# A transformer encoder on one core: a new cost table and a new rating for the planner that fixes every engine's order

## The chip, the cores and the metric

The kernel runs on one core of a Trainium2 chip. A core has five engines that each take their instructions strictly in the order of the program: PE (TensorE, the matrix engine, with PEld for its weight loads), DVE (VectorE), ACT (ScalarE), POOL (GpSimd) and SP (SyncE, which here only issues transfers). They run beside each other and wait for each other by semaphores. The metric is the device time of one execution in microseconds (us).

## The reference

Two transformer layers on 512 tokens of width 1024, all in float32. Layer 0 mixes tokens by two-dimensional neighbourhood attention, layer 1 by three groups of dilated windowed attention whose outputs are merged by their softmax denominators. Both layers then have a SwiGLU block of hidden width 2816.

```python
for layer in range(DEPTH):                       # DEPTH = 2
    h = rms_norm(x, norm_mix_pre[layer])
    if layer % 2 == 0:
        h = neighbourhood_attention(h, na_w_qkv[j], na_w_o[j], na_rpb[j])
    else:
        h = dilated_attention(h, dil_w_qkv[j], dil_w_o[j])
    x = x + rms_norm(h, norm_mix_post[layer])
    h = rms_norm(x, norm_ffn_pre[layer])
    x = x + rms_norm((silu(h @ w_gate) * (h @ w_up)) @ w_down, norm_ffn_post[layer])
```

## The kernel before

A float32 matrix product is made of three products in the faster type float32r: each operand is split into a high part, `h`, and a remainder, `l` (function `split`, lines 370 to 373: ACT copies the operand to `h` at line 371, DVE subtracts it to get `l` at line 372). `mm3` (lines 381 to 387) then issues `h` by `h` (line 383), `h` by `l` (line 384) and `l` by `h` (line 385). Nearly all of PE's work is on these three lines. The large products are done by a scheme of seven block products instead of eight (class `Seven`, from line 418), whose sums of weights are made on POOL and DVE (lines 451 to 457) and whose results ACT and DVE collect from the accumulators. A row of the profile such as `gu<-rxa,h_b` is a matmul of the gate and up product (`gate_up`), `yd` one of the down product (`down`), `yo` one of the output projection, `vp` and `vd` make the values, `pp` queries and keys, `tr` are transposes of the normalized tokens (lines 599 to 608: four transposes on PE, then ACT at line 607 and DVE at line 608 copy high part and remainder), `s`, `sa`, `sb` are attention scores and `o` their products with the values.

The stages follow each other in time: tokens and values of layer 0, its attention heads (to about 210 us), output projection (to 255 us), gate and up product (to about 490 us), down product (to 593 us), values of layer 1 (to about 705 us), its heads (to about 1080 us), output projection, gate and up, down (to the end).

The order on every engine is not the order in which the code is written. When all instructions are recorded, class `Order` builds the graph of what must wait for what, plays the program through with a table of durations (`_cost`: how long an instruction keeps its engine and how long until its result is there; transfers share one pipe) and takes at each moment the ready instruction of lowest rank (`run`). `pin` repeats this forward and backward eight times, each turn with the ranks of the last, keeps the turn whose played end is earliest, and ties every engine's instructions together in that order (`add_manual_dep`). On the chip each engine then follows its list: if the head of the list waits, all behind it wait too. SP's and POOL's transfers are in such lists as well.

## Time and profile before

| | us |
|---|---|
| three runs, lowest, median, highest | 1476.14, 1478.42, 1480.89 |
| the profiled execution | 1475.85 |
| its span, first to last instruction | 1474.0 |
| PE busy | 1425.7 (97%) |
| DVE busy | 1200.5 (81%) |
| ACT busy | 902.7 (61%) |
| POOL busy | 541.4 (37%) |

The profiled execution is the one from which all durations are read; 1.85 us of its time lie around its span. A row of the timeline gives start and length of an instruction, and in brackets how long its engine had been idle before it and whose result ended the wait. The ends of matmuls are modelled: in a run of matmuls of 256 columns the starts are 0.113 us apart, while each is drawn as about 0.28 us long. An idle time of PE is therefore one that is seen beyond that overlap.

### The profile page before, as it was taken

The page shows a single profiled execution, that of the slowest core. Times are in us where ns is not written, and L with a number is a line of the kernel's source. Part 1 is how long each engine was busy: PE and PEld are TensorE (multiplying, and loading weights), DVE is VectorE, ACT ScalarE, POOL GpSimd, SP SyncE. Part 2 cuts the span into 40 slices and gives each one's busy share as a digit, 9 for nine tenths or more (in the row PEclk, how much of TensorE's full clock was granted, in tenths as well). Part 3 has the DMA queues.
Part 4 walks back from the last instruction along what each step waited for, and adds up shares of the span by engine and source line. Part 5 has one row for each costly group of instructions (what it writes and reads, how often), then busy time and mean ns, then how long its engine had stood idle before and what let it go on. Part 6 is the DMA issues. An engine that isn't in the chain of part 4 may idle for free.

```text
span 1474.0 us, 27934 instructions
## 1 busy us (share of the span) xinstructions
PE 1425.7 (97%) x10788; PEld 1317.0 (89%) x10788; DVE 1200.5 (81%) x1876; ACT 902.7 (61%) x1819; POOL 541.4 (37%) x398
## 2 busy tenths in 40 slices
PE   7999999899999999999999999999999999999997
PEld 7988877899999888999999999989877999999886
DVE  5489976799999788797789788787656989998877
ACT  4478773555555567544467777876675655555664
POOL 5345424644231001566555443334303743330001
PEclk9999999999999999999999999999999999999999
DMA  5356578778333664435433243343665688844662
GB/s 201 133 181 166 164 254 220 257 207 233 115 111 116 206 223 165 159 128 196 139 106 99 86 147 108 108 135 102 221 203 219 207 222 263 262 150 151 192 218 97
DMA packets 86645, 253.22 MB, mean 172 GB/s; under 512 B 19312, under 2 KB 31600, under 8 KB 84464
## 3 DMA queue, kind: packets, MB, share of 16 engines
q1 hardware_dynamic: 77696, 197.69, 40.4%
q0 software_dynamic: 8672, 53.48, 14.0%
q8 instruction: 85, 1.39, 0.4%
q14 instruction: 48, 0.39, 0.1%
q10 hardware_dynamic: 144, 0.26, 0.0%
HBM read 229.24 MB, written 68.29 MB: 202 GB/s over the span
## 4 chain that ended last, share of the span: by engine, by line
PE 66%; DVE 15%; ACT 8%; DMA 4%; issue 4%; POOL 1%; SPq 0%; POOLq 0%; DVEq 0%; ACTq 0%
PE gu L383 7%; PE gu L384 7%; PE gu L385 7%; PE pp_d L383 4%; PE pp_d L385 4%; PE pp_d L384 3%; PE yd_s L385 3%; PE yd_s L384 3%; PE yd_s L383 3%; PE yd_pp L384 2%; PE yd_pp L385 2%; PE yd_pp L383 2%; PE yo L383 2%; PE yo L385 1%; PE yo L384 1%
## 5 line engine op out<-in xcount | busy, mean ns | idle before, releaser
L591 POOL TENSOR_TENSOR rs_yd<-v_yd,mhalf 128x1 f32<-128x1 f32 x8 | 9.5, 1184 | 255.2 <-DVE v_yd L589 255.2
L383 PE MATMUL gu<-rxa,h_c 128*128 128x256 f32 x352 | 99.3, 282 | 3.1 <-DVE memc L845 1.4
L384 PE MATMUL gu<-rxa,h_b 128*128 128x256 f32 x352 | 98.9, 281 | 2.2 <-DVE rxa L608 2.2
L383 PE MATMUL gu<-rxc,h_a 128*128 128x256 f32 x352 | 97.7, 279 | 2.4 <-ACT h_a L371 1.5
L383 PE MATMUL gu<-rxa,h_b 128*128 128x256 f32 x352 | 98.6, 281 | 1.2 <-ACT rxa L607 1.2
L384 PE MATMUL gu<-rxc,h_a 128*128 128x256 f32 x352 | 98.0, 279 | 1.1 <-DVE rxc L608 1.0
L385 PE MATMUL gu<-rxa,l_b 128*128 128x256 f32 x352 | 98.6, 280 | 0.3 <-DVE l_b L372 0.3
L384 PE MATMUL gu<-rxa,h_c 128*128 128x256 f32 x352 | 97.5, 277 | 0.0
L385 PE MATMUL gu<-rxc,l_a 128*128 128x256 f32 x352 | 97.3, 277 | 0.0
L385 PE MATMUL gu<-rxa,l_c 128*128 128x256 f32 x352 | 97.1, 277 | 0.0
L371 ACT ACTIVATE rxc<-mem 128x512 fp32r<-128x512 f32 (+2 forms) x90 | 55.7, 624 | 62.7 <-PE yd_pp L384 31.6
L451 POOL TENSOR_TENSOR r_d<-r_d 128x512 f32<-128x512 f32 x24 | 33.4, 1391 | 162.2 <-DVE l_ad L372 123.5
L451 POOL TENSOR_TENSOR r_gu<-r_gu 128x512 f32<-128x512 f32 x20 | 29.8, 1488 | 148.9 <-DVE l_a L372 105.8
L372 DVE TENSOR_TENSOR rxc<-mem,rxc 128x512 fp32r<-128x512 f32 (+2 forms) x90 | 64.3, 717 | 17.3 <-ACT rxc L371 17.1
L451 POOL TENSOR_TENSOR raw<-raw 128x512 f32<-128x512 f32 x24 | 40.3, 1678 | 94.0 <-DVE l_a L372 66.6
L383 PEld LDWEIGHTS gu<-rxa,h_c 128*128 128x128 f32 x352 | 66.1, 188 | 5.9 <-DVE memc L847 2.0
L384 PEld LDWEIGHTS gu<-rxa,h_b 128*128 128x128 f32 x352 | 67.3, 191 | 2.4 <-DVE rxa L608 2.4
L383 PEld LDWEIGHTS gu<-rxc,h_a 128*128 128x128 f32 x352 | 65.9, 188 | 3.4 <-ACT h_a L371 2.1
L1244 ACT ACTIVATE mem<-mem 128x256 f32<-128x256 f32 x128 | 63.7, 503 | 8.1 <-DVE mem L1243 7.9
L383 PEld LDWEIGHTS gu<-rxa,h_b 128*128 128x128 f32 x352 | 67.0, 191 | 1.6 <-ACT rxa L607 1.4
L384 PEld LDWEIGHTS gu<-rxc,h_a 128*128 128x128 f32 x352 | 66.2, 188 | 1.8 <-DVE rxc L608 1.8
L385 PEld LDWEIGHTS gu<-rxa,l_b 128*128 128x128 f32 x352 | 67.3, 191 | 0.5 <-DVE l_b L372 0.5
(609 smaller groups left out, 6149.6 us busy)
## 6 DMA issues: line engine op xcount, KB each, us to landing
wsum<-wd POOLq DMA_DIRECT2D x24, 1408.0 KB, 11.9
r_d<-dil_qk SPq DMA_DIRECT2D x48, 512.0 KB, 4.1
raw<-wg SPq DMA_DIRECT2D x24, 512.0 KB, 5.7
raw<-wu SPq DMA_DIRECT2D x24, 512.0 KB, 8.2
wsum<-wsum POOLq DMA_DIRECT2D x8, 1408.0 KB, 9.1
raw<-wsum SPq DMA_DIRECT2D x22, 512.0 KB, 4.1
r_gu<-wg SPq DMA_DIRECT2D x20, 512.0 KB, 3.8
r_gu<-wu SPq DMA_DIRECT2D x20, 512.0 KB, 5.8
```

Source lines behind the costliest of these rows:

```text
L371: act.activation(h, src, AF.Copy)
L372: dve.tensor_sub(l, src, h.bitcast(F32))
L383: i = pe.matmul(o, s[0], m[0], start=start, stop=False, skip_group_check=True)
L384: pe.matmul(o, s[0], m[1], start=False, stop=False, skip_group_check=True)
L385: pe.matmul(o, s[1], m[0], start=False, stop=stop, skip_group_check=True)
L451: self.added = e[0].tensor_add(q[0], q[0], q[2])
L591: pool.tensor_tensor(r, v, mhalf, op=ALU.pow)
L1244: act.activation(pr[:, f], pr[:, f], AF.Exp, bias=st[:, c:c + 1], scale=-1.0, accum_out=st[:, c + 2:c + 3])
```

## The change

The change is in the planner alone; no instruction is added or taken away (PE 10,388 matmuls, DVE 1,878 rows, ACT 1,582, SP 520 transfers in both programs).

- `_cost`: a float32r matmul of n columns keeps PE for 17n/38.4 + 3 ns instead of n/2.4 + 13 ns: 116.3 instead of 119.7 for 256 columns, 229.7 instead of 226.3 for 512.
- `access`: two writes of one engine to ranges that interleave, less than 12 instructions apart, keep their written order.
- `usual` is new: it plays a finished order strictly (every engine takes its list as it stands) three times, each time with landings of transfers drawn at random and small random delays of all other results, and returns the mean end.
- `pin` makes 14 turns instead of 8, rates each by `usual` instead of by its one played end, and then goes through the program in stretches of 100 us: in each it tries the ranks of the eight next best turns for that stretch, and keeps them when the rating falls.

```diff
@@ -87,13 +88,12 @@
     if t == "InstDMACopy":
         adds = "bypass" not in str(getattr(i, "cce_op", "bypass"))
         size = 4 * n * outs[0].ap[0][1] * (1.78 if adds else 1)
-
-        return 350 if e == 4 else 1000 if adds else 560, LATE if size < 2e4 else 0, e == 3, 0, size
+        return 350 if e == 4 else 1000 if adds else 560, 0, e == 3, 0, size
     if e == 0:
         if i.is_transpose:
             return (109, 240, False, 1, 0) if srcs[1].ap[0][1] == P else (202, 330, False, 2, 0)
         if str(srcs[0].dtype).endswith("float32r"):
-            return n / 2.4 + 13, n / 2.4 + 175, False, 0, 0
+            return n * 17 / 38.4 + 3, n * 17 / 38.4 + 175, False, 0, 0
 
         upper = outs[0].offset >= HD * 512 if outs[0].ap[0][1] == HD else srcs[1].offset >= HD * srcs[1].tensor.shape[1]
         return 0.75 * n + 15, 1.67 * n + 200, False, 4 if upper else 3, 0
@@ -171,7 +171,9 @@
                 if bank and (self.engine[m] or self.engine[n]):
                     self.pred[n].add(m)
                 elif q0 < p1 and p0 < q1 and lo2 < hi and lo < hi2 and \
-                        any(x < d and c < y for x, y in runs for c, d in runs2):
+                        (any(x < d and c < y for x, y in runs for c, d in runs2) or
+
+                         write and wrote and self.engine[m] == self.engine[n] and n - m < 12):
                     self.pred[n].add(m)
                     if write and len(runs) == 1 and p0 <= q0 and q1 <= p1 and lo <= lo2 and hi2 <= hi:
                         continue
@@ -218,7 +220,7 @@
             for m in before:
                 self.succ[m].append(n)
 
-    stay = 1000.0
+    stay, strict = 1000.0, False
 
     def run(self, rank, back):
 
@@ -242,8 +244,10 @@
                 heap = min((q for q in heaps[e] if q), key=lambda q: q[0])
 
                 for q in heaps[e][3:] if kind == 3 else heaps[e][kind:kind + 1]:
-                    if e == 0 and q and q[0][0] < heap[0][0] + self.stay:
+                    if e == 0 and not self.strict and q and q[0][0] < heap[0][0] + self.stay:
                         heap = q
+                if self.strict and heap[0][0] != len(order[e]):
+                    continue
                 k = heapq.heappop(heap)[1]
                 taken, later, lock, mode, size = self.costs[k]
                 s = max(now, locked[5 - e]) if lock else now
@@ -278,20 +282,54 @@
                 now = min(q[0] if q is wake else q[0][0] for q in (wake, pending) if q)
         return starts, order, max(s + max(c[1], c[4] and LANDING + c[4] / RATE) for s, c in zip(starts, self.costs))
 
-    def pin(self, tc, times):
-        rank, best = list(range(len(self.all))), None
+    def usual(self, order):
+
+        planned, place, ends = self.costs, [0] * len(self.all), []
+        for q in order:
+            for p, k in enumerate(q):
+                place[k] = p
+        self.strict = True
+        for seed in range(3):
+            r = random.Random(seed)
+            self.costs = []
+            for e, (taken, later, lock, mode, size) in zip(self.engine, planned):
+                if size:
+                    later = r.gauss(300, 700) if size < 4e5 else r.gauss(50, 800)
+                    later *= 1.6 if e == 3 else 1
+                else:
+                    later += r.expovariate(1 / 15)
+                self.costs.append((taken, later, lock, mode, size))
+            ends.append(self.run(place, False)[2])
+        self.costs, self.strict = planned, False
+        return sum(ends) / len(ends)
+
+    def pin(self, tc, times, span):
+        rank, found = list(range(len(self.all))), []
+
+        self.costs = [(t, LATE if 0 < size < 2e4 else later, lock, mode, size) for t, later, lock, mode, size in self.costs]
         for _ in range(times):
             starts, order, end = self.run(rank, False)
-            if best is None or end < best[0]:
-                best = end, order
+            found.append((self.usual(order), end, rank, starts, order))
             starts, _, end = self.run([-s - c[1] for s, c in zip(starts, self.costs)], True)
             rank = [end - s - c[0] for s, c in zip(starts, self.costs)]
-        for q in best[1]:
+        found.sort(key=lambda f: f[0])
+
+        best, end, rank, base, order = found[0]
+        for lo in np.arange(0.0, max(base), span):
+            part = [k for k, s in enumerate(base) if lo <= s < lo + span]
+            for _, _, other, _, _ in found[1:9]:
+                mixed, shift = list(rank), float(np.median([rank[k] - other[k] for k in part]))
+                for k in part:
+                    mixed[k] = other[k] + shift
+                _, new, e = self.run(mixed, False)
+                usual = self.usual(new) if e < end + 3000 else best
+                if usual < best:
+                    best, end, rank, order = usual, e, mixed, new
+        for q in order:
             for m, n in zip(q, q[1:]):
                 tc.add_manual_dep(self.all[n], self.all[m].name,
                                   mybir.DependencyInfo(mybir.DependencyClass.NoSync, mybir.DependencyReason.DATA),
                                   reason="order")
-        return best[0]
 
 
 @with_exitstack
@@ -1444,7 +1482,7 @@
               for n, lo, hi, o, c, side in arenas]
     order = Order(tc.nc.cur_bb.bb.instructions)
     order.link(tags, places, extra)
-    order.pin(tc, 8)
+    order.pin(tc, 14, 1e5)
 
 
 def _blocks(w, cols):
```

Lines of the kernel after stand 38 higher from `encoder_kernel` on: line 372 of before is line 410 there, 608 is 646, 845 is 883, 1318 is 1356.

Where the orders differ: half of PE's instructions stand within 4 places of where they stood, nine tenths within 23; on DVE half within 1 and nine tenths within 6. Counted along PE's two lists, the neighbours of different kind (float32r matmul, transpose, float32 matmul) are 433 before and 415 now. The following are three places of it.

DVE at the start of the gate and up product of layer 0. `tr_o0_3_4` is a transposed operand of the fourth token tile, whose remainder the next matmuls of PE need; `l_b0_1` and `l_c0_1` are remainders of weights; the row of `memc` between them in before (line 842) collects a result. Before:

```order
L372 TENSOR_TENSOR l_c0_0_3079<-r_gu0_0_2857,h_c0_0_3078 128x1024
L608 TENSOR_TENSOR rxa_77<-tr_o0_3_3_2809,rxa_77 128x4x128
L441 MEMSET gu0_1_2895 128x256
L372 TENSOR_TENSOR l_b0_1_3101<-r_gu0_1_2892,h_b0_1_3100 128x1024
L842 TENSOR_TENSOR memc0_2852<-memc0_2852,gu0_2_2929 128x256
L372 TENSOR_TENSOR l_c0_1_3161<-r_gu0_1_2892,h_c0_1_3160 128x1024
L608 TENSOR_TENSOR rxa_77<-tr_o0_3_4_2817,rxa_77 128x4x128
L441 MEMSET gu0_2_2929 128x256
L842 TENSOR_TENSOR memc0_2852<-memc0_2852,gu0_3_2963 128x256
```

and now:

```order
L410 TENSOR_TENSOR l_c0_0_3079<-r_gu0_0_2857,h_c0_0_3078 128x1024
L646 TENSOR_TENSOR rxa_77<-tr_o0_3_3_2809,rxa_77 128x4x128
L646 TENSOR_TENSOR rxa_77<-tr_o0_3_4_2817,rxa_77 128x4x128
L410 TENSOR_TENSOR l_b0_1_3101<-r_gu0_1_2892,h_b0_1_3100 128x1024
L880 TENSOR_TENSOR memc0_2852<-memc0_2852,gu0_2_2929 128x256
L410 TENSOR_TENSOR l_c0_1_3161<-r_gu0_1_2892,h_c0_1_3160 128x1024
L646 TENSOR_TENSOR rxa_77<-tr_o0_3_5_2825,rxa_77 128x4x128
L479 MEMSET gu0_2_2929 128x256
```

The copy of `tr_o0_3_4` moved ahead of the two weight remainders and the collected result between them. On PE the four transposes that it copies moved too: they stood directly ahead of the first matmul that reads them, and now stand 21 matmuls ahead of it.

DVE in the gate and up product of layer 1, at the eighth of its 22 units. The rows that write `memc1` from `gu1_8` collect a result, after which PE may go on in that accumulator. Before:

```order
L372 TENSOR_TENSOR l_a1_12_13729<-raw1_12538,h_a1_12_13728 128x1024
L845 TENSOR_TENSOR memc1_12534<-memc1_12534,gu1_8_13248 128x256
L372 TENSOR_TENSOR vmem_80<-r_gu1_10_13478,vmem_80 128x512
L372 TENSOR_TENSOR l_c1_9_13775<-raw1_12538,h_c1_9_13774 128x1024
L847 TENSOR_TENSOR memc1_12534<-mem_79,gu1_8_13248 128x256
L453 TENSOR_TENSOR r_gu1_10_13478<-r_gu1_10_13478 128x512
L842 TENSOR_TENSOR memc1_12534<-memc1_12534,gu1_11_13598 128x256
```

and now:

```order
L889 TENSOR_TENSOR mem_79<-memc1_12534,mem_79 128x2x256
L883 TENSOR_TENSOR memc1_12534<-memc1_12534,gu1_8_13248 128x256
L410 TENSOR_TENSOR l_a1_12_13729<-raw1_12538,h_a1_12_13728 128x1024
L410 TENSOR_TENSOR vmem_80<-r_gu1_10_13478,vmem_80 128x512
L885 TENSOR_TENSOR memc1_12534<-mem_79,gu1_8_13248 128x256
L491 TENSOR_TENSOR r_gu1_10_13478<-r_gu1_10_13478 128x512
L410 TENSOR_TENSOR l_c1_9_13775<-raw1_12538,h_c1_9_13774 128x1024
```

The row that writes `memc1` from `mem` and `gu1_8` moved ahead of the remainder `l_c1_9`; the row of line 845 (now 883), which collects from the same accumulator into `memc1`, moved in the same way ahead of `l_a1_12`.

SP in the heads of layer 1. `vd0` are stored values that are loaded into a buffer which the heads' last products with the values free; `r_d19` are the weights of a later unit; `sw` are small exchanges of softmax sums. Before:

```order
L1204 DMA sw0_6414<-mem_79 128x16
L1206 DMA mem_79<-sw2_6416 32x4x4
L367 DMA r_d19_10688<-dil_qk 128x1024
L1206 DMA mem_79<-sw2_6416 32x4x4 x3
L367 DMA r_d19_10688<-dil_qk 128x1024
L1206 DMA mem_79<-sw0_6414 32x4x4 x4
L1318 DMA mem_79<-vd0_6418 128x4x256
L1318 DMA mem_79<-vd1_6419 128x1024
```

and now:

```order
L1287 DMA memc0_2852<-dil_bias 128x512
L1242 DMA sw2_6416<-mem_79 128x16
L1356 DMA mem_79<-vd0_6418 128x4x256
L1287 DMA memc0_2852<-dil_bias 128x512
L405 DMA r_d19_10688<-dil_qk 128x1024
L1242 DMA sw0_6414<-mem_79 128x16
L1244 DMA mem_79<-sw2_6416 32x4x4 x4
L405 DMA r_d19_10688<-dil_qk 128x1024
L1244 DMA mem_79<-sw0_6414 32x4x4 x4
```

The load of `vd0` moved from behind both loads of `r_d19` to ahead of them. PE's products with the values that free its buffer (lines 1349 and 1355) moved ahead as well, from behind the matmuls of units 15 to 17 to ahead of them.

## Rows read from the trace of the kernel before

**Rows 1.** The page of the profile: busy time and its share of the span by engine.

```profile
span 1474.0 us, 27934 instructions
PE 1425.7 (97%) x10788; PEld 1317.0 (89%) x10788; DVE 1200.5 (81%) x1876; ACT 902.7 (61%) x1819; POOL 541.4 (37%) x398
```

**Rows 2.** The timeline of PE: the first transposes, and the last matmul (start, length, what, and in brackets the idle time before it).

```profile
7.91 1.97 PE L605 MATMUL tr_a<-ident,mem 128*128 128x128 f32 x8 [7.91 <-DVE mem L598]
...
1465.51 0.39 PE L385 MATMUL yd_s<-h_d1x2b,rxc 128*128 128x512 f32 x1
```

**Rows 3.** The timeline of PE from 276 to 289 us, the start of the gate and up product of layer 0.

```profile
276.16 0.28 PE L383 MATMUL gu<-rxc,h_a 128*128 128x256 f32 x1
276.27 0.28 PE L384 MATMUL gu<-rxc,h_a 128*128 128x256 f32 x1
...
278.20 0.60 PE L605 MATMUL tr_o<-ident,mem 128*128 128x128 f32 x4
279.96 0.50 PE L383 MATMUL gu<-rxa,h_b 128*128 128x256 f32 x2 [1.16 <-ACT rxa L607]
282.69 0.58 PE L384 MATMUL gu<-rxa,h_b 128*128 128x256 f32 x1 [2.23 <-DVE rxa L608]
283.07 0.42 PE L385 MATMUL gu<-rxa,l_b 128*128 128x256 f32 x1
...
288.62 0.30 PE L384 MATMUL gu<-rxa,h_b 128*128 128x256 f32 x1
```

**Rows 4.** The timeline of DVE from 278 to 283 us.

```profile
278.43 1.39 DVE L372 TENSOR_TENSOR l_b<-r_gu,h_b 128x1024 fp32r<-128x1024 f32 x1
279.74 0.41 DVE L842 TENSOR_TENSOR memc<-memc,gu 128x256 f32<-128x256 f32 x1
280.07 1.96 DVE L372 TENSOR_TENSOR l_c<-r_gu,h_c 128x1024 fp32r<-128x1024 f32 x1
281.96 0.68 DVE L608 TENSOR_TENSOR rxa<-tr_o,rxa 128x512 fp32r<-128x512 f32 x1
```

**Rows 5.** The stretch from 282 to 289 us: length, busy time of PE, PEld, DVE, ACT and POOL, then PE's granted clock as a share of full speed, the share of the DMA engines and GB/s.

```profile
282.00:289.00 7.00, 6.31 (x30) 6.31 (x31) 2.78 (x8) 1.44 (x4) 3.51 (x4) 0.53 0.87 298
```

**Rows 6.** The timeline of ACT from 255 to 263 us: the split of a weight that waits for its transfer.

```profile
261.54 1.06 ACT L371 ACTIVATE h_a<-raw 128x1024 fp32r<-128x1024 f32 x1 [1.83 <-DMA raw<-wg]
```

**Rows 7.** Waits of PE in the two gate and up products, from its timeline.

```profile
366.09 0.38 PE L383 MATMUL gu<-rxa,h_c 128*128 128x256 f32 x1 [0.66 <-DVE memc L845]
...
424.42 0.39 PE L383 MATMUL gu<-rxa,h_c 128*128 128x256 f32 x1 [0.42 <-DVE memc L845]
...
472.62 0.38 PE L383 MATMUL gu<-rxa,h_c 128*128 128x256 f32 x1 [0.31 <-DVE mem L845]
...
1245.30 0.39 PE L383 MATMUL gu<-rxa,h_c 128*128 128x256 f32 x1 [1.25 <-DVE memc L847]
```

**Rows 8.** The timeline of DVE ahead of the last of these waits.

```profile
1242.61 2.31 DVE L372 TENSOR_TENSOR l_c<-raw,h_c 128x1024 fp32r<-128x1024 f32 x1
1244.84 0.41 DVE L847 TENSOR_TENSOR memc<-mem,gu 128x256 f32<-128x256 f32 x1
```

**Rows 9.** The timeline in the heads of layer 1, first PE, then DVE.

```profile
959.59 0.39 PE L383 MATMUL pp_d<-rxb,h_cd 128*128 128x256 f32 x1 [1.05 <-DVE mem L689]
...
978.42 0.36 PE L383 MATMUL pp_d<-rxb,h_bd 128*128 128x256 f32 x1 [0.94 <-DVE pp_d L441]
...
975.67 1.87 DVE L372 TENSOR_TENSOR l_cd<-r_d,h_cd 128x1024 fp32r<-128x1024 f32 x1 [0.46 <-ACT h_cd L371]
```

**Rows 10.** The timeline of PE and of DVE at the end of the down product of layer 0.

```profile
593.46 0.36 PE L383 MATMUL vp_d<-h_d,rxa 128*128 128x256 f32 x1
593.66 0.28 PE L384 MATMUL vp_d<-l_d,rxa 128*128 128x256 f32 x1
593.78 0.28 PE L385 MATMUL vp_d<-h_d,rxa 128*128 128x256 f32 x1
...
598.26 0.39 PE L384 MATMUL vp_d<-l_d,rxa 128*128 128x256 f32 x1 [2.03 <-DVE l_d L372]
...
598.12 0.68 DVE L643 TENSOR_TENSOR memc<-yd_s,mem 128x512 f32<-128x512 f32 x1
```

**Rows 11.** The timeline of PE at the end of the heads of layer 1.

```profile
1056.75 0.38 PE L385 MATMUL pp_d<-rxb,l_bd 128*128 128x256 f32 x1 [0.44 <-DVE l_bd L372]
```

**Rows 12.** Two stretches of the gate and up products, columns as in rows 5 (DVE's busy time is the third).

```profile
300.00:350.00 50.00, 50.00 (x443) 50.00 (x442) 48.16 (x55) 25.72 (x45) 26.12 (x18) 1.00 0.84 242
...
1300.00:1350.00 50.00, 49.57 (x423) 48.83 (x422) 48.21 (x65) 27.60 (x49) 13.94 (x8) 1.00 0.37 123
```

**Rows 13.** Line 372 on DVE in the gate and up product of layer 0 (255 to 490 us), by tile: count, shortest, median and longest in ns, first and last start, shape.

```profile
L372 DVE TENSOR_TENSOR l_a<-raw,h_a x12: 1208/1218/1886, 262.6 to 432.4; 128x1024 fp32r<-128x1024 f32 x12
L372 DVE TENSOR_TENSOR l_b<-raw,h_b x12: 1199/1222/2506, 294.4 to 461.8; 128x1024 fp32r<-128x1024 f32 x12
L372 DVE TENSOR_TENSOR l_c<-raw,h_c x12: 1211/2016/2316, 302.3 to 463.9; 128x1024 fp32r<-128x1024 f32 x12
L372 DVE TENSOR_TENSOR l_b<-r_gu,h_b x10: 1202/1226/1391, 272.9 to 474.4; 128x1024 fp32r<-128x1024 f32 x10
```

**Rows 14.** The timeline of SP from 948 to 966 us: its DMA issues (the length is that of the issue).

```profile
953.89 0.38 SPq L367 DMA_DIRECT2D r_d<-dil_qk  x1
...
962.30 2.34 SPq L1318 DMA_DIRECT2D mem<-vd  x3
```

More of the change, by code (lines that the diff above doesn't have):

```diff
@@ L1 @@
 import heapq
+import random
 from contextlib import ExitStack, contextmanager
```

## The prediction

> **What bounds the kernel now.** I read the page first, then PE's timeline, and only then what PE waits for. The page says that PE is busy 1425.7 of 1474.0 us and that DVE, the next engine, has 1200.5 [rows 1]. PE's first instruction starts at 7.91 us and its last matmul ends at 1465.51 + 0.39 = 1465.90 [rows 2], so its idle time between the two is 1465.90 - 7.91 - 1425.7 = 32.3 us. The change leaves every instruction as it is. It can therefore win at most these 32.3 us, and what PE loses at its half clock after long waits. The order within that is all that moves, so the right question is which of PE's waits the new order takes away, and which it makes.
>
> The largest loss is one place, the start of the gate and up product of layer 0. PE waits 1.16 us at 279.96 for ACT, runs two matmuls, and waits 2.23 us at 282.69 for DVE [rows 3]. From 282 to 289 us the granted clock is 0.53, that is the level of 1.2 GHz, behind waits of 3.39 us in sum [rows 5]. The waits in the two gate and up products are of one kind: DVE collects an accumulator (lines 845 and 847) later than PE wants it back [rows 7]. In the last of them DVE was busy with a remainder of 2.31 us before it took the 0.41 us of line 847 [rows 8]. Others stand in the heads of layer 1 [rows 9] and at the end of the down product [rows 10].
>
> **The change, part by part.** All durations are of the one profiled execution: 1475.85 us, 1474.0 of them its span. The median of the three runs is 1478.42, which is 2.57 more; I make the sum against the profiled execution and add 2.57 at the end.
>
> *The start of gate and up, layer 0.* Line 608 for `tr_o0_3_4` started at 281.96, right behind `l_b` (1.39 us), line 842 (0.41) and `l_c` (1.96), 3.76 us of work [rows 4]. Now all three stand behind it, and the four transposes stand 21 matmuls earlier on PE; at 0.11 us a matmul [rows 3] that is 2.3 us, more than the 1.16 us that PE waited for ACT's copy. Both waits go: -3.39. The half clock goes with them, if it was the waits that brought it. From 283.07 to 288.62 PE did 25 matmuls and four transposes in 5.55 us; at full clock these are 25 x 0.11 + 0.60 = 3.35 [rows 3], so another -2.2. Against it: the third unit's first matmuls on `h_a` now stand ahead of eight others that filled PE's wait for that weight. ACT has it at 261.54 + 1.06 = 262.60, released by a transfer [rows 6], and no order makes a transfer earlier; eight matmuls of 0.11 us are +0.9. Together -4.7. The bounds are -5.6 (the eight are hidden) and -1.2 (a wait of 1.3 us remains for the next operand, and the clock falls all the same: -3.39 + 1.3 + 0.9). What is late next: DVE's two remainders, by the 0.68 us of line 608, for matmuls that stand further on.
>
> *Collecting in gate and up, both layers.* The rows of lines 845 and 847 that PE waited for now stand ahead of the weight remainders: 0.66 + 0.42 + 0.31 + 1.25 [rows 7] = -2.6. What hides the remainder's delay of 0.41 us is that it belongs to a unit several matmul groups later; if that cover is gone, the same 0.41 comes back at each place, 1.6 in all. Bounds -2.6 and -1.0.
>
> *Heads of layer 1.* The 0.94 us at 978.42 are a wait for DVE's clearing of `pp_d` (line 441), which stood behind `l_cd`, 1.87 us from 975.67. It now stands ahead of it. The 1.05 us at 959.59 wait for line 689 [rows 9]; 20 matmuls of unit 15 now stand ahead of the waiting one. Together -2.0, bounds -2.0 and 0.
>
> *End of the down product, layer 0.* PE waits 2.03 us for `l_d` [rows 10]. DVE now does line 643 (0.68 us) and one copy of a transpose ahead of `l_d`, while its chain starts some 0.4 us earlier. I keep the wait and count +0.3, bounds -0.5 and +1.4.
>
> *End of the heads.* At 1056.75 PE waits 0.44 for `l_bd` [rows 11]. PE's own work ahead of it shrinks by 2.0 us, DVE's only by the 0.6 us of one row that moved behind: +1.4, bounds 0 and +1.4.
>
> *Changes of kind.* Between matmuls of different kind the starts were 0.20 us apart instead of 0.12 [rows 10]. There are 433 such neighbours before and 415 now: 18 x 0.08 = -1.4 at most. Some lie where PE waits anyway, so I take -1.0.
>
> *The extra rule in `access`* only keeps written orders; it holds back no instruction that PE waits for in these places: 0. *The rest of the order* has small waits that go and others that come. I have priced 10.5 of 32.3 us of idle time; for the other 21.8 I take no change, and a tenth, 2.2 us, to either side.
>
> Sum: -4.7 - 2.6 - 2.0 + 0.3 + 1.4 - 1.0 = -8.6, so 1475.85 - 8.6 = 1467.25 on the profile's scale and 1469.8 on that of the median. I forecast 1470. The bounds added up are -5.6 - 2.6 - 2.0 - 0.5 - 1.4 - 2.2 = -14.3 and -1.2 - 1.0 + 1.4 + 1.4 + 2.2 = +2.8, that is 1464 to 1481.
>
> **The rivals.** *The waits only move.* A wait taken away on PE can come back at the next place, since the transfers and DVE have not become faster; then the idle time stays at 32 us and the time at about 1478. For it speaks that more than half of PE's instructions stand within four places of where they stood, and that DVE in the gate and up products has only 50 - 48.16 = 1.84 us free in 50 [rows 12]. Against it speaks that at 279 to 289 us the engine that was waited for had its work in the wrong order, not too much of it: DVE was busy 2.78 of the 7 us [rows 5].
>
> *SP's queue.* The load of `vd0` now stands ahead of both loads of `r_d19`. Before, it was issued at 962.30, and the first `r_d19` at 953.89 [rows 14]. If `vd0` waits for its buffer as long as before, `r_d19` comes 8.4 us late and all its users with it. PE's products that free the buffer moved ahead, so I take half, 4.2 us, and a stretch at half clock as above, 2.2: 1470 + 6.4 = 1476.4. This counts as no change.
>
> *The slower case: DVE becomes the bound in gate and up.* There DVE has 1.84 and 1.79 us free in 50 [rows 12], so over the 475 us of both products about 17 us. Remainders of one shape take 1.22 us in the median for `l_a` and `l_b` and 2.02 for `l_c` from `raw` [rows 13]: 0.8 us more, which I read as two engines that meet, POOL being busy 26 of these 50 us [rows 12]. The new order moves such pieces against POOL. There are 34 of the short kind in one product, 68 in both [rows 13]. If 40 of them turn long, DVE gets 32 us more work, 15 more than it has free. The 2.6 us of collecting then don't come: 1469.8 + 2.6 + 15 = 1487. It is slower than before from 17 + 8.6 - 2.6 = 23 us of added work, or 29 pieces. Against it: nothing in the order brings these rows nearer to POOL's, and they moved by one place in the median.
>
> The Trainium skill, "SBUF — State Buffer", section "Who interferes with whom", gives a rule for this: VectorE and GpSimd share a port pair that is locked, not shared out, and whoever starts first keeps it for its whole instruction; its section on the two sides of SBUF names a VectorE instruction with two SBUF inputs among those that take it. The trace agrees as far as two lengths of one instruction go, 1.22 and 2.02 us; that the lock is their cause no row here shows. By that rule a change of order alone can lengthen work that nobody added, and the time would be that of the slower case.
>
> *More goes.* If a third of the 21.8 us that I left unpriced goes too, the time is 1470 - 7 = 1463.
>
> **How the numbers follow.** The forecast has 0.54, more goes 0.10, the waits only move 0.16, SP's queue 0.07, DVE as the bound 0.08, and 0.05 are left for new waits behind which the clock falls elsewhere. What a measurement of this kernel can tell from no change is 0.3%, 4.4 us: faster is below 1474.0, slower above 1482.9. Faster has 0.54 + 0.10 = 0.64, the same 0.16 + 0.07 = 0.23, slower 0.13. The forecast's own range is 1464 to 1474. The range of 8 in 10 reaches on the one side below the case of more, on the other to the upper bound of the sum, which takes in both cases of no change: 1460 to 1481.
>
> **What would show it.** Right, step by step: no wait over 0.5 us between 276 and 290 us and a granted clock of 1.00 there; the waits for lines 845 and 847 (now 883 and 885) gone from the gate and up products; that for line 441 (now 479) in the heads of layer 1 gone; one of about 1.8 us near 1050; DVE's busy time in the two products unchanged; PE's idle time between first and last instruction near 25 us. Wrong: `r_d19` split late, and PE waiting for it; DVE over 49 us busy in 50 with more remainders at 2 us; or the same 32 us of idle time with other names on it.

## The result, and the profile of the changed kernel

The changed kernel took 1468.56 us in the median of four runs (1467.52 to 1470.22), the kernel before 1477.30 in the median of its four. The ratio is 0.9937 with an interval of 0.992 to 0.9955: faster by 0.6%, about 9 us. The forecast was 1470, with 1460 to 1481 around it. Measured once more, beside the kernel before and the last orders tried below, it gave the same ratio again (0.9937, 0.9918 to 0.9957).

The page of the profile after, head and engines; PE's first and last instruction from its timeline (start, length, and in brackets the idle time before):

```profile
span 1468.4 us, 27943 instructions
...
PE 1427.6 (97%) x10788; PEld 1323.3 (90%) x10788; DVE 1190.6 (81%) x1876; ACT 902.6 (61%) x1819; POOL 550.5 (37%) x398
```

```profile
7.96 0.90 PE L643 MATMUL tr_a<-ident,mem 128*128 128x128 f32 x3 [7.96 <-DVE mem L636]
...
1459.83 0.39 PE L423 MATMUL yd_s<-h_d1x2b,rxc 128*128 128x512 f32 x1
```

Against [rows 1, 2], PE's last matmul ends at 1460.22 instead of 1465.90. Idle between first and last instruction is 1460.22 - 7.96 - 1427.6 = 24.7 us, where it was 32.3. So 7.6 us of waits are gone, and the prediction had "near 25". But PE is *busier* by 1.9 us with the same 10,788 instructions, and the profiled execution is only 1475.85 - 1470.22 = 5.6 us shorter. Something lengthened PE's work; the part on the unexpected comes back to it.

The waits of PE over 0.9 us that the trace after has behind 500 us, with the shorter ones right beside them:

```profile
585.79 0.39 PE L421 MATMUL vp_d<-h_d,rxa 128*128 128x256 f32 x1 [0.71 <-ACT rxa L645]
586.71 0.66 PE L643 MATMUL tr_n<-ident,mem 128*128 128x128 f32 x4 [0.42 <-DVE rxa L646]
590.23 0.38 PE L422 MATMUL vp_d<-l_d,rxa 128*128 128x256 f32 x1 [1.13 <-DVE v_n L625]
...
787.76 0.36 PE L421 MATMUL pp_d<-rxb,h_bd 128*128 128x256 f32 x1 [0.98 <-DVE pp_d L479]
...
796.23 0.39 PE L423 MATMUL pp_d<-rxa,l_ad 128*128 128x256 f32 x1 [1.12 <-DVE l_ad L410]
...
1124.76 0.66 PE L643 MATMUL tr_o<-ident,mem 128*128 128x128 f32 x4 [1.18 <-DVE rxc L646]
1125.96 0.66 PE L643 MATMUL tr_o<-ident,mem 128*128 128x128 f32 x4 [0.54 <-DVE rxc L646]
1127.44 0.58 PE L421 MATMUL gu<-rxc,h_a 128*128 128x256 f32 x1 [0.59 <-ACT h_a L409]
1129.11 0.58 PE L422 MATMUL gu<-rxc,h_a 128*128 128x256 f32 x1 [1.09 <-DVE rxc L646]
...
1174.06 0.38 PE L421 MATMUL gu<-rxc,h_a 128*128 128x256 f32 x1 [1.18 <-ACT h_a L409]
```

Between 260 and 585 us PE has no wait over 0.3 us left, and nothing at lines 883 and 885 [rows 7] is in the list. What is new stands at the start of the gate and up product of layer 1, from 1124 to 1130 us. The windows of the trace after (length, busy time of PE, PEld, DVE, ACT, POOL, then PE's granted clock) put both starts side by side, and under them the two whole products:

```profile
255.00:490.00 235.00, 232.31 (x1947) 228.85 (x1946) 212.53 (x274) 131.48 (x228) 88.61 (x57) 1.00 0.59 183
1115.00:1355.00 240.00, 234.29 (x1927) 230.27 (x1926) 208.28 (x272) 128.93 (x225) 94.70 (x66) 0.99 0.68 201
282.00:289.00 7.00, 7.00 (x63) 7.00 (x63) 5.90 (x11) 5.08 (x10) 0.00 (x0) 1.00 0.99 337
1122.00:1136.00 14.00, 10.61 (x62) 9.46 (x61) 10.33 (x14) 7.91 (x14) 9.92 (x8) 0.76 0.74 263
```

From 282 to 289 us PE does 63 instructions at a clock of 1.00, where it did 30 at 0.53 [rows 5]. The half clock has not gone from the program, though: it stands at 1127.5 us now, behind the new waits, where the kernel before had only 0.74 and 0.49 us of waiting and full clock:

```profile
1137.55 0.51 PE L383 MATMUL gu<-rxc,h_a 128*128 128x256 f32 x2 [0.74 <-ACT rxc L607]
...
1138.99 0.38 PE L384 MATMUL gu<-rxc,h_a 128*128 128x256 f32 x1 [0.49 <-DVE rxc L608]
```

Where the time went by stage, of the two profiled executions, worked out from the starts of PE's instructions. A stage ends where the next one's first work on PE stands (in gate and up the transposes ahead of it, elsewhere its first product), so the cuts lie at other times in the two:

| stage | idle before, after | slow pace before, after | half clock before, after | length after less before |
|---|---|---|---|---|
| layer 0 to its output projection | 7.3, 7.2 | 3.3, 3.7 | 0, 0 | -1.5 |
| gate and up, down, layer 0 | 8.0, 2.7 | 1.1, 4.4 | 2.6, 0 | -6.3 |
| values of layer 1 | 4.0, 2.3 | 1.8, 4.2 | 1.6, 0 | -5.4 |
| heads of layer 1, output projection | 9.2, 6.8 | 4.3, 5.0 | 0, 0 | +1.5 |
| gate and up, down, layer 1 | 3.8, 5.7 | 1.7, 5.8 | 0, 2.5 | +5.9 |

"Slow pace" is time by which matmuls that follow each other without a wait start up to 20 ns later than 113.3 ns (256 columns) or 226.7 ns (512) after the one before; it was not in the prediction at all, and it rises in each stage. At its first work on gate and up in layer 1 the changed kernel was 11.6 us ahead; the last stage gave back 5.9 of them. The cuts are not of equal work: in the stage of the heads the changed kernel has 26 more of PE's instructions, some 3 us of products of the values that came ahead of that cut before.

### The profile page after: what moved, and what is told of

It is laid out like the page before. It is cut to its first block, busy times and chain, and to the rows that moved or that the text cites. A ratio compares the mean times of both kernels' runs of the same rounds, so it can differ in the third digit from the quotient of the medians.

```text
span 1468.4 us, 27943 instructions
## 1 busy us (share of the span) xinstructions
PE 1427.6 (97%) x10788; PEld 1323.3 (90%) x10788; DVE 1190.6 (81%) x1876; ACT 902.6 (61%) x1819; POOL 550.5 (37%) x398
## 4 chain that ended last, share of the span: by engine, by line
PE 83%; DVE 6%; ACT 6%; DMA 2%; issue 2%; POOL 1%; POOLq 0%; SPq 0%; DVEq 0%; ACTq 0%
PE gu L421 9%; PE gu L422 9%; PE gu L423 9%; PE pp_d L421 5%; PE pp_d L422 5%; PE pp_d L423 4%; PE yd_s L421 3%; PE yd_s L423 3%; PE yd_s L422 3%; PE vd L421 2%; PE vd L422 2%; PE vd L423 2%; PE yd_pp L423 2%; PE yd_pp L421 2%; PE yd_pp L422 2%
## 5 line engine op out<-in xcount | busy, mean ns | idle before, releaser
L629 POOL TENSOR_TENSOR rs_yd<-v_yd,mhalf 128x1 f32<-128x1 f32 x8 | 13.2, 1655 | 259.3 <-DVE v_yd L627 259.3
L421 PE MATMUL gu<-rxc,h_a 128*128 128x256 f32 x352 | 100.0, 285 | 2.9 <-ACT h_a L409 2.8
L422 PE MATMUL gu<-rxc,h_a 128*128 128x256 f32 x352 | 99.6, 283 | 1.1 <-DVE rxc L646 1.1
L410 DVE TENSOR_TENSOR rxc<-mem,rxc 128x512 fp32r<-128x512 f32 (+2 forms) x90 | 66.9, 749 | 17.4 <-ACT rxc L409 17.3
L423 PEld LDWEIGHTS gu<-rxc,l_a 128*128 128x128 f32 x352 | 67.9, 193 | 0.0
L501 ACT ACTIVATE mem<-gu 128x256 f32<-128x256 f32 x44 | 16.9, 383 | 82.9 <-PE gu L423 78.4
## 6 DMA issues: line engine op xcount, KB each, us to landing
wsum<-wd POOLq DMA_DIRECT2D x24, 1408.0 KB, 12.1
```

The lines of the kernel that those rows point to most:

```text
L410: dve.tensor_sub(l, src, h.bitcast(F32))
L421: i = pe.matmul(o, s[0], m[0], start=start, stop=False, skip_group_check=True)
L422: pe.matmul(o, s[0], m[1], start=False, stop=False, skip_group_check=True)
L423: pe.matmul(o, s[1], m[0], start=False, stop=stop, skip_group_check=True)
L501: act.activation(self.p5, self.right, AF.Copy)
L629: pool.tensor_tensor(r, v, mhalf, op=ALU.pow)
```

## The experiments

**The two kernels once more, to see what belongs to the order and what to one execution.** No edit.

> The changed kernel once more, with a second profile of it. In the first, matmuls of 256 columns that follow each other without a wait start either 113.3 ns or 117.8 ns apart, in long stretches of the one or the other; the slower ones cost 20.8 us in sum there, and 10.0 in the profile of before, with the same matmuls. If the pace of a stretch is set by the order of the program, the second profile has the slow stretches at the same places (308 to 404 us, 626 to 713 us, 1200 to 1350 us) and again 20 to 22 us in sum. If it is drawn anew at each interruption, the stretches differ and the sum moves by several us. Time 1467 to 1471 either way.

> The kernel of before once more, with a second profile. If the pace of matmuls is set by the order, the cost of the slower pace is again 10.0 us (9 to 11) and 300 to 450 us is again at 113.3 ns; if it is drawn anew, the sum is anywhere between 5 and 20 us and the span moves with it. The half clock at 282 and 599 us and the waits ahead of it (1.16 and 2.23; 2.03) should come again, within 0.2 us.

The changed kernel took 1468.74 us in its second profile, the kernel before 1482.80. PE's timeline in the second profile of before, at the waits of [rows 3, 7]:

```profile
279.51 0.50 PE L383 MATMUL gu<-rxa,h_b 128*128 128x256 f32 x2 [1.16 <-ACT rxa L607]
...
282.39 0.58 PE L384 MATMUL gu<-rxa,h_b 128*128 128x256 f32 x1 [2.38 <-DVE rxa L608]
...
1246.18 0.39 PE L383 MATMUL gu<-rxa,h_c 128*128 128x256 f32 x1 [1.09 <-DVE memc L845]
```

The start of gate and up is the same within 0.2 us, and so is the half clock behind it (2.6 and 2.4 us lost): these come with the order. (The expectation's 10.0 and 20.8 us count only the clearly slow steps of 256 columns; counted as in the table by stage they are 12.1 and 23.0.) Of the four waits for lines 845 and 847, 2.64 us in sum, this execution has one, 1.09. They belong to the execution that I happened to read. At the first of them, 366.09 us, it is DVE that differs. The rows ahead of it in the profile of [rows 7]:

```profile
364.48 1.23 DVE L372 TENSOR_TENSOR l_a<-raw,h_a 128x1024 fp32r<-128x1024 f32 x1 [0.50 <-ACT h_a L371]
365.62 0.41 DVE L845 TENSOR_TENSOR memc<-memc,gu 128x256 f32<-128x256 f32 x1
```

and in the second profile, with PE's matmul:

```profile
363.53 1.21 DVE L372 TENSOR_TENSOR l_a<-raw,h_a 128x1024 fp32r<-128x1024 f32 x1
364.67 0.41 DVE L845 TENSOR_TENSOR memc<-memc,gu 128x256 f32<-128x256 f32 x1
...
365.13 0.39 PE L383 MATMUL gu<-rxa,h_c 128*128 128x256 f32 x1
```

DVE did not wait 0.50 us for ACT and collected 0.95 us earlier; PE was there earlier too, at 365.13 against 366.09 - 0.66 = 365.43. At the next, 424.42 us, it is PE: it came 1.0 us later in the second profile and DVE 0.6, so the accumulator had been collected. PE's pace had slowed between them, as the windows from 350 to 400 us show, first of the profile of [rows 7], then of the second profile of before (with 300 to 350):

```profile
350.00:400.00 50.00, 49.34 (x434) 49.13 (x433) 47.97 (x59) 26.65 (x47) 15.92 (x11) 1.00 0.51 145
```

```profile
300.00:350.00 50.00, 50.00 (x443) 50.00 (x442) 48.33 (x56) 26.04 (x46) 26.51 (x18) 1.00 0.86 242
350.00:400.00 50.00, 49.92 (x429) 49.72 (x429) 47.40 (x60) 27.26 (x48) 15.72 (x10) 1.00 0.51 147
```

With fewer waits (49.92 busy against 49.34) the second does *fewer* instructions in the same 50 us, 429 against 434. The pace of matmuls cost 12.1 us in the first execution of before and 21.7 in the second, of the same program. So the guess that it is set by the order alone falls. It isn't drawn freely either: the changed kernel had 23.0 and 22.1 (and 25.1 in a third, below), and its matmuls from 626 to 711 us go at the slow pace each time.

**The start of gate and up alone.** The order of before with six rows moved (four transposes on PE, one copy each on ACT and DVE); `_moved`, new at the end of the file, takes the named instructions out of an engine's list and puts them ahead of another.

```diff
-        for q in best[1]:
+        for q in _moved(self, best[1]):
...
+MOVES = [([2818, 2819, 2820, 2821], 3004), ([2822], 2992), ([2823], 3103)]
```

On PE this is

```
 L383 MATMUL gu0_4_2997<-rxc,h_a0_4_2998 128x256
 L384 MATMUL gu0_4_2997<-rxc,h_a0_4_2998 128x256
+L605 MATMUL tr_o0_3_4_2817<-ident,mem 128x128 x4
 L385 MATMUL gu0_4_2997<-rxc,l_a0_4_2999 128x256
```

and the copies on ACT and DVE move ahead in the same way.

> The order of before, with the new order's moves at the start of the gate and up product of layer 0 alone: the four transposes tr_o0_3_4 21 matmuls earlier on PE, their copies earlier on ACT and DVE. The prediction's term: both waits (3.4 us) and the half clock (2.2 us) go, without the 0.9 for the third unit's weight, which isn't moved here: -5.6 us, ratio 0.9962. Rival, the waits only move: the next operand or weight is waited for, and the time is that of before within 1 us, ratio 1.000. If the waits go and the half clock stays: -3.4 us.

Measured: 0.9981 (0.9966 to 0.9997), that is 2.8 us of 1480.2, between 0.4 and 5.0. Less than the 5.6 expected, and more than nothing. PE's timeline, and its window of [rows 5]:

```profile
262.12 0.39 PE L383 MATMUL gu<-rxc,h_a 128*128 128x256 f32 x1 [1.94 <-ACT h_a L371]
```

```profile
276.13 0.65 PE L605 MATMUL tr_o<-ident,mem 128*128 128x128 f32 x4 [0.65 <-POOL mem L631]
...
285.12 0.38 PE L383 MATMUL gu<-rxa,vmem 128*128 128x256 f32 x1 [1.84 <-ACT mem L463]
```

```profile
282.00:289.00 7.00, 5.09 (x43) 4.69 (x42) 4.35 (x10) 2.89 (x7) 3.14 (x3) 1.00 0.95 323
```

The wait at 262.12 is for the weight's transfer, outside the moved rows; it was 1.35 us in the first execution of before and 0.66 in the second. Both waits at 280 and 283 us and the half clock are gone. In place of the 3.39 us come 0.65 (the transposes, placed earlier, now wait for the tokens that POOL's line 631 writes) and 1.84 (an accumulator that ACT's line 463 copies out). The rows behind the second:

```profile
280.91 1.98 DVE L372 TENSOR_TENSOR l_c<-r_gu,h_c 128x1024 fp32r<-128x1024 f32 x1
...
283.13 0.72 DVE L842 TENSOR_TENSOR memc<-memc,gu 128x256 f32<-128x256 f32 x2
...
283.56 0.74 ACT L849 ACTIVATE memc<-memc 128x256 f32<-128x256 f32 x2 [2.12 <-DVE memc L842]
...
284.69 0.38 ACT L463 ACTIVATE mem<-gu 128x256 f32<-128x256 f32 x1
```

ACT sat idle for 2.12 us until DVE, behind its two remainders `l_b` (2.07 us here) and `l_c`, had done line 842, and the copy of line 463 stands behind that in ACT's list. The rival of waits that only move was right for three quarters of the two waits, the prediction for the clock. In the changed kernel neither wait comes; its order has other rows around the move.

**The collecting alone.**

```diff
-        for q in best[1]:
+        for q in _moved(self, best[1]):
...
+MOVES = [([3959], 4049), ([4653], 4742), ([5602], 5315), ([13641], 13731), ([13674, 13795], 13777)]
```

For the first pair this is, on DVE,

```
 L851 TENSOR_TENSOR mem<-memc0_2852,mem 128x2x256
+L845 TENSOR_TENSOR memc0_2852<-memc0_2852,gu0_8_3566 128x256
 L372 TENSOR_TENSOR l_a0_12_4047<-raw0_2856,h_a0_12_4046 128x1024
-L845 TENSOR_TENSOR memc0_2852<-memc0_2852,gu0_8_3566 128x256
```

At the wait of 472.62 us it is a row of line 942 that moves, from ahead of the collecting row to behind it, and with the row of line 847 a sum of line 453 goes along: six rows in all, not the five of the expectation.

> The order of before, with the rows of lines 845 and 847 ahead of the weight remainders in the two gate and up products (five rows of DVE moved, nothing on the other engines). The prediction's term: the waits of 0.66, 0.42, 0.31 and 1.25 us go and nothing takes their place, -2.6 us, ratio 0.9982. Rival, the remainders that now come later are waited for: -1.0 us or nothing, ratio 0.9993 to 1.000. If the pace of matmuls is drawn at each interruption, the time may move by a few us either way beyond that.

Measured: 0.9988 (0.9975 to 1.0002), 1.8 us of 1480.2, between a gain of 3.7 and a loss of 0.3. In its profile none of the four waits is there; the one other wait of PE over 0.3 us near them is

```profile
476.08 0.39 PE L383 MATMUL gu<-rxa,h_b 128*128 128x256 f32 x1 [0.48 <-ACT h_b L371]
```

for a high part that ACT makes; the remainders that come later are not waited for. The interval doesn't tell 2.6 from 1.0 us, and the second profile of before says why 2.6 is the upper end. The two places that were moved alone give 2.8 and 1.8 us, of the 8.7 us between the medians; the rest is read from the ledger below, and no run moved it alone.

**The parts of the planner.** Each takes one thing of the change away, or does it alone:

```diff
-            return n / 2.4 + 13, n / 2.4 + 175, False, 0, 0
+            return n * 17 / 38.4 + 3, n * 17 / 38.4 + 175, False, 0, 0
```

is all that the first has beside the kernel before; the second is the changed kernel with this line taken back; the third and the fourth are the changed kernel with

```diff
-        for lo in np.arange(0.0, max(base), span):
+        for lo in []:
```

and with

```diff
-        for seed in range(3):
+        for seed in range(3, 6):
```

> The kernel of before with the new duration of float32r matmuls alone: 8 turns, the old choice by one played end, no stretches, no extra rule. If the durations carry the gain, ratio 0.993 to 0.996 against before; if the rating and its stretches carry it, 0.998 to 1.002, with a wait of over 1 us and a half clock left in the gate and up product's start of layer 0 or 1.

> The changed kernel with the old duration of float32r matmuls (119.7 instead of 116.3 ns for 256 columns); rating, turns, stretches and extra rule as changed. If the rating carries the gain: ratio 0.992 to 0.996, PE's idle time between first and last instruction 23 to 27 us. If the durations carry it: 0.998 to 1.002, idle time 29 to 33 us.

> The changed kernel without the stretches: 14 turns, the one of the best rating is taken whole. If choosing by the rating is enough: ratio 0.992 to 0.996. If the stretches carry it: 0.997 to 1.001, and PE's idle time is 28 to 32 us. My own guess is between, 0.995 to 0.998.

> The changed kernel, its rating drawn from three other seeds, so that another order is taken by the same rule. If the rule is what helps, ratio 0.990 to 0.996 and idle time 22 to 27 us. If the order taken was a lucky one, 0.996 to 1.002 and 27 to 32 us.

| order | ratio to before | interval |
|---|---|---|
| durations alone | 0.9947 | 0.9927 to 0.9967 |
| the change with the old durations | 0.9930 | 0.9905 to 0.9955 |
| the change without the stretches | 0.9932 | 0.9910 to 0.9954 |
| the change with three other seeds | 0.9892 | 0.9870 to 0.9914 |

Each part gives nearly the whole gain by itself, so the parts don't add. The stretches bring nothing that can be seen: 0.9932 without them, 0.9937 with them; my guess of 0.995 to 0.998 for that run was wrong. And three other seeds, the same rule, give an order that is 0.45% better than that of the change, with no overlap of the intervals. This asks for a rival that I hadn't stated ahead of these runs: each part merely draws a new order, and that of before was a poor draw.

**Other draws.** The old planner with a duration shorter by 1 ns, and with more turns; the new one with six plays to a rating; and the changed kernel beside them.

```diff
-            return n / 2.4 + 13, n / 2.4 + 175, False, 0, 0
+            return n / 2.4 + 12, n / 2.4 + 175, False, 0, 0
```

```diff
-    order.pin(tc, 8)
+    order.pin(tc, 14)
```

```diff
-        for seed in range(3):
+        for seed in range(6):
```

> The kernel of before with float32r matmuls shorter by 1 ns in the cost table (118.7 instead of 119.7 ns for 256 columns), nothing else: 8 turns, the old choice. This is no better measurement of them (the trace has 113.3 or 117.8), but another draw of the order. If the durations of the change (116.3) helped because they are truer, this order is as good as that of before or a third of the way to it: ratio 0.998 to 1.002. If the order of before was a poor draw and almost any other is better: 0.992 to 0.996.

> The kernel of before with 14 turns instead of 8, the old durations and the old choice by one played end. Another order is taken. If the old choice picks well, more turns make it better or leave it: ratio 0.995 to 1.000. If it is a poor guide and orders scatter by half a per cent: anywhere from 0.991 to 1.004. If the order of before was a poor draw: 0.992 to 0.996.

> The changed kernel, each order rated by six random plays (seeds 0 to 5) instead of three. If the rating orders its candidates rightly and three plays are too few, ratio 0.987 to 0.991, as good as the run with the other three seeds or better. If the rating doesn't tell orders of this quality apart: 0.990 to 0.996, as the changed kernel.

> The changed kernel beside these, on the same chip, to compare them with. Ratio 0.992 to 0.9955 as in the result. Third profile of it: if the pace of matmuls is drawn anew in each execution, long stretches at 113.3 ns lie elsewhere than in the first two; PE's idle time between first and last instruction 23 to 25 us again.

| order | ratio to before | interval |
|---|---|---|
| old choice, shorter by 1 ns | 1.0028 | 1.0015 to 1.0042 |
| old choice, 14 turns | 0.9950 | 0.9930 to 0.9970 |
| new choice, six seeds | 0.9884 | 0.9864 to 0.9903 |
| the changed kernel | 0.9937 | 0.9918 to 0.9957 |

A nanosecond less makes an order that is slower than before, so the kernel before was no especially poor draw. The old choice by one played end takes orders from 0.9947 to 1.0028, 0.8% apart; the five that were chosen by the rating lie between 0.9884 and 0.9937, all of them below all four of the old choice, if narrowly: the intervals of 0.9937 and 0.9947 overlap. That speaks for the rating as what carries the gain, and the durations alone and the 14 turns as lucky draws of the old choice, with four and five orders as all the evidence. A rival stands beside it: all five rated orders were taken from 14 turns, and the only order of the old choice that was, 0.9950, can't be told from the one with the same durations and the rating, 0.9930. No run has the rating with 8 turns, and none takes the rule in `access` away alone. The rating in turn takes better orders with six plays than with the three of the change. On one chip the six seeds took 1461.16 us against 1470.28 of the changed kernel: the order that beats both kernels, by 0.6% once more. Its page:

```profile
span 1457.6 us, 27923 instructions
...
PE 1421.4 (98%) x10788; PEld 1317.6 (90%) x10788; DVE 1196.3 (82%) x1876; ACT 901.8 (62%) x1819; POOL 541.5 (37%) x398
```

The ledger of all executions, worked out as in the table by stage; "late starts" are matmuls that start over 20 ns late beyond any idle time:

| execution | idle | slow pace | late starts | half clock |
|---|---|---|---|---|
| before, first and second profile | 32.3, 30.2 | 12.1, 21.7 | 31.2, 29.2 | 4.1, 5.6 |
| start alone, collecting alone | 32.1, 31.3 | 18.9, 23.4 | 30.1, 28.3 | 0, 2.7 |
| shorter by 1 ns | 33.2 | 19.6 | 28.5 | 0 |
| durations alone, 14 turns | 25.9, 25.7 | 16.4, 18.4 | 22.6, 26.9 | 3.2, 3.1 |
| changed, three profiles | 24.6, 23.3, 23.8 | 23.0, 22.1, 25.1 | 23.3, 22.1, 23.1 | 2.5, 4.4, 1.5 |
| old durations, no stretches | 26.7, 22.0 | 21.2, 21.9 | 27.4, 24.5 | 3.2, 3.0 |
| other seeds, six seeds | 22.9, 20.3 | 17.4, 19.4 | 23.6, 22.7 | 3.0, 0 |

Idle time follows the verdicts: over 30 us in the four slow orders, 20 to 27 in the fast ones.

## Why the prediction was right

The time, 1470 against 1468.56, and the way to it, waits that go because DVE has its work in another order, were right. Several terms were not, and that they add up to the time is in part luck. The forecast had -5.4 us of waits, -2.2 of half clock and -1.0 of changes of kind. The first profiles of the two kernels differ by -7.6 of idle time, -1.6 of half clock, -7.9 of late starts and +10.9 of slow pace: that is -6.2, against -5.6 between the two profiled executions. The last two were, but for the -1.0, not in the sum, and they nearly cancel.

- *The start of gate and up, -4.7.* At the place it came as worked out: no wait, clock 1.00, the 1.35 us of the third unit's weight still there as 1.04 at 259.54. (Between 283.07 and 288.62 us stand 22 matmuls and not 25 [rows 3], so the half clock cost 5.55 - 22 x 0.11 - 0.60 = 2.5 us and not 2.2.) But alone it is worth 2.8 us, since 0.65 and 1.84 us come back further on; the sum priced one place as if the next had nothing late. The step "what is late next: two remainders" had the right rows and the wrong way: PE did not wait for them but for an accumulator whose copy on ACT stood behind them, and for POOL's tokens.
- *Collecting, -2.6.* The waits went, and the cover over the remainders held. The size was that of one execution: another of before has 1.09 of the 2.64. Nor does the order rule out every wait of this kind. In the third profile of the changed kernel there is one, behind a piece of DVE that took 0.69 us in the first profile:

```profile
405.61 1.82 DVE L410 TENSOR_TENSOR rxc<-r_gu,rxc 128x512 fp32r<-128x512 f32 x1
...
407.82 0.39 PE L421 MATMUL gu<-rxa,h_c 128*128 128x256 f32 x1 [0.79 <-DVE mem L883]
```

- *Heads of layer 1, -2.0.* The two waits are gone, but two of the same kind came, 0.98 for line 479 at 787.76 and 1.12 at 796.23. Idle time of that stage with its projection fell by 2.4 all the same.
- *End of the down product, +0.3.* 0.71 + 0.42 + 1.13 = 2.26 in place of 2.03 [rows 10]: +0.23, near the number but not by the step. The wait for `l_d`, which was to stay, is gone, and three others stand in its place. That the half clock there would go, 1.6 us, I had not counted.
- *End of the heads, +1.4.* Wrong: there is no wait. Two rows of PE show why:

```profile
1042.92 0.28 PE L421 MATMUL pp_d<-rxb,h_bd 128*128 128x256 f32 x1
...
1043.37 0.36 PE L423 MATMUL pp_d<-rxb,l_bd 128*128 128x256 f32 x1
```

PE begins on the unit with matmuls on `h_bd` and puts others between, and `l_bd`, which DVE starts at 1042.06 and has after 1.23 us, is there at 1043.29. The step looked at what moved ahead of the matmul, and not at what moved to stand between.
- *Changes of kind, -1.0, 1.4 at most.* Near in size, though not by its count. By the three kinds named, both traces and both lists have 345 such neighbours before and 350 after, not 433 and 415; a product of `mm3` has something else beside it 383 times before and 355 after. What was read as the cost of a change, 0.20 us instead of 0.12 [rows 10], stands between two products of which the first is right behind transposes; late starts at such places fell from 134 to 126, by 0.7 us. What the sum lacks is the other late starts; all of them together fell by 7.9 us (31.2 to 23.3). Of these, 3.2 lie at waits, 43 before and 22 after: a wait costs about 0.17 us more than its idle time shows. 2.3 lie at the product right behind one that waited (41 and 19 starts, about 0.1 us late without idle time), and 1.7 within runs (75 and 54).
- *The rest of the order, 0 +- 2.2.* This is the step that failed. At the start of gate and up of layer 1 idle time rose from 1.23 us (0.74 and 0.49 above) to 3.40 (the four waits from 1124.76), and 2.5 us of half clock came with it; the 0.05 for "new waits behind which the clock falls elsewhere" was too little for a mechanism that did come, inside a faster kernel.
- *From the profiled execution to the median, +2.57.* For the kernel before the four runs give 1.45; in the changed kernel the profiled execution lay 1.66 above the median. The term hides the largest of all: PE's pace, at which the profiled execution of before had lost 12.1 us, and the second of it and the three of the changed kernel 22 to 25.

The rivals: *the waits only move* fell with 24.6, 23.3 and 23.8 us of idle time instead of 32.3 and 30.2. *SP's queue* fell: SP issues the first `vd0` at 943.95 and the two `r_d` behind it at 946.18 and 949.77, where the first of them had been issued at 953.89 [rows 14], with the products that free the buffer placed earlier; PE has no wait over 0.3 us from 841 to 982 us.

```profile
943.95 0.38 SPq L1356 DMA_DIRECT2D mem<-vd  x1
...
946.18 0.33 SPq L405 DMA_DIRECT2D r_d<-dil_qk  x1
...
949.77 0.43 SPq L405 DMA_DIRECT2D r_d<-dil_qk  x1
```

*DVE as the bound* fell too. In the two products of before DVE was busy 208.30 and 218.88 us,

```profile
255.00:490.00 235.00, 226.97 (x1915) 223.06 (x1914) 208.30 (x267) 128.89 (x223) 87.80 (x58) 0.99 0.56 176
1115.00:1355.00 240.00, 236.20 (x1942) 229.40 (x1942) 218.88 (x283) 130.34 (x235) 98.50 (x71) 1.00 0.70 211
```

427.2 us against 420.8 after (in the whole program 1200.5 and 1190.6, with the same 1,876 instructions). So DVE had 475 - 427.2 = 47.8 us free, not the 17 us that the two fullest stretches [rows 12] suggest, and the 32 us of 40 lengthened pieces would not have filled it. The pieces that were long are long still (`l_c` from `raw` has a median of 2.25 us after, 2.02 before [rows 13]) and the short ones short:

```profile
L410 DVE TENSOR_TENSOR l_b<-raw,h_b x12: 1201/1222/2117, 286.2 to 454.3; 128x1024 fp32r<-128x1024 f32 x12
L410 DVE TENSOR_TENSOR l_c<-raw,h_c x12: 1212/2254/2316, 293.5 to 456.4; 128x1024 fp32r<-128x1024 f32 x12
```

What the Trainium skill ("SBUF — State Buffer", section "Who interferes with whom") says of the locked port pair is neither confirmed nor contradicted by that; no run here took POOL's work away.

## What to carry to other kernels

When a planner fixes the order, price a change by the places where the longest waits stand, but take the next operand that is late into the sum before believing a place's whole price: here three quarters of two waits came back when that place alone was mended. Rate an order by several disturbed plays rather than by one undisturbed end; the choice by one end scattered by 0.8% when a matmul's duration in the table was 1 or 3.4 ns shorter, and twice as many plays were worth another 0.6%, though three others were worth nearly as much, so that a part of it is the draw, and what the 14 turns do without the rating rests on one order. Profile the same program twice before sizing small waits: which of them an execution shows depends on when each of the two engines comes to them.

## What was not expected of the hardware

The same matmuls, float32r with 256 columns, run at two paces at full clock: starts 113.3 ns or 117.8 ns apart, for hundreds of them in a row. An interruption (a wait, a transpose between) may change the pace, and the stretch behind it mostly keeps it; one execution spends 2,400 to 5,300 of its 7,300 to 7,450 such steps at the slower one. It shows in the windows as the number of instructions in 50 us of unbroken work: 443 from 300 to 350 us before [rows 12], and in the changed kernel, first, second and third profile, and with six seeds:

```profile
300.00:350.00 50.00, 50.00 (x430) 50.00 (x429) 43.73 (x55) 25.80 (x46) 23.07 (x16) 1.00 0.95 252
```

```profile
300.00:350.00 50.00, 50.00 (x429) 50.00 (x428) 43.62 (x56) 25.69 (x45) 23.24 (x17) 1.00 0.94 252
```

```profile
300.00:350.00 50.00, 50.00 (x427) 50.00 (x426) 43.20 (x56) 25.70 (x45) 22.88 (x17) 1.00 0.93 249
```

```profile
300.00:350.00 50.00, 50.00 (x444) 50.00 (x443) 44.35 (x59) 26.55 (x46) 19.44 (x15) 1.00 0.92 245
```

PE is busy without a gap and at a clock of 1.00 in all four, and does 427 to 430 or 444 instructions. What decides between the paces stays open: no run changed it on purpose, and it is partly the order's (this stretch is slow in three of three profiles of the changed kernel) and partly the execution's (12.1 and 21.7 us for one program). The Trainium skill, "TensorE: Matmul & The Clock Gate", section "Back-to-back issue gap", says that in a stream of weight loads and matmuls both set the spacing; its isolated figure for 256 columns, 262 cycles or 109 ns at 2.4 GHz, is shorter than either pace here, and the measurement decides.

The half clock is as particular. In the order of before it came behind 1.16 and 2.23 us of waiting with 2 matmuls between, and in the changed kernel behind four waits of 0.5 to 1.2 us; in the run with the start alone it did not come behind a wait of 1.84. Nor do the same waits always bring it. In the changed kernel PE waits 1.41 and 1.04 us between 252 and 260 us in all three profiles, and the clock from 256 to 262 us was 1.00, 0.72 and 1.00. With the collecting alone moved, the waits of 1.16 and 2.30 us at 280 and 282 us were those of before, and the clock from 282 to 289 us was 0.76 instead of 0.53. So a term for the half clock at one place is worth some 1.5 us either way from one execution to the next, and the length of a wait alone does not tell whether it comes.
